# A list scheduler that bounds its stretches of small TensorE products by a time, and then keeps to full ones for a while

## The chip, the cores and the metric

The kernel runs on one core of one Trainium2 chip. The metric is the device time of one execution in microseconds; what stands for a kernel is the median of several runs. The five engines with a queue of their own are TensorE (PE in the profile, with the weight loads as PEld), VectorE (DVE), ScalarE (ACT), GpSimd (POOL) and SyncE (SP), which here only issues transfers.

## The reference

All data are float32, with one batch of 512 positions of width 1024. Two transformer layers follow each other:

```python
x = first_block(x, c, ...)        # adaLN; sparse attention + latent attention, gated; MLP, d_ff 4096
# second_block:
h = rmsnorm_2(x, norm_mix_g)
proj = h @ w_in                                          # 512 + 3*512 columns
y_ssm = s5_mixer(proj[..., :512], ...)                   # state-space scan, then a GLU
y_att = chunked_attention(q, k, v, rel_bias)             # 8 heads of 64
mixed = concat(rmsnorm_2(y_ssm, g1), rmsnorm_2(y_att, g2))
x = x + mixed @ w_out
h2 = rmsnorm_2(x, norm_ffn_g)
x = x + (silu(h2 @ w_gate) * (h2 @ w_up)) @ w_down       # d_ff 2816
return rmsnorm_2(x, norm_final_g)
```

The `s5_mixer` has 32 groups of 16 channels with 64 complex states each:

```python
bu = einsum('bsgh,gph->bsgp', uf, b_bar)
_, states = associative_scan(combine, (lam_bar, bu), axis=1)
y = einsum('bsgp,ghp->bsgh', states, c_mat).real + d_skip * uf
y = gelu(y); y = y * sigmoid(y @ w_glu + b_glu)
```

## The kernel before

**How products are made.** A large matrix product is kept at float32's precision by splitting both sides into a high and a low part (`hh`, `hl` for activations; `wh`, `wl` for weights) and adding three products: high by high, low by high, high by low. Weights stream through a ring of four buffers: a transfer on SP's queue brings a piece `wr` of 128x1024, ACT casts it to `wh`, and `Weights.low` (line 463) makes `wl = wr - wh`, on DVE, or on an engine that the scheduler chooses between DVE and POOL (`vg`). When `wl` is made, `Weights.freed` issues the transfer of the piece four further on, so that this transfer stands in SP's queue until that subtraction is done.

**The scan of the second block.** `ssm(hf)` (line 1990) is called for two halves of the channels. It loads 14 tables `rec` and the inputs `U`, makes for each of two sets `o` a bank T of 16 products with 64x64 tables (T<-U), which use a quarter of TensorE's array each, scans the result on DVE (`sr`, `st`, `ss`), and then makes two banks Y: 8 products T<-U of the full 128-row tables with 64 columns of output width and 16 products T<-ss, which contract over 64 rows only. These last and the 64x64 ones are called small here; PE's tiling then is (64, 64) or (64, 128) and not the full (128, 128). ACT copies the banks to `ye`; eight transfers on SP write it to `yd` in memory, two read it back transposed as `yt`, ACT copies each to `yy`, and a gelu follows on ACT and DVE (`yq`, `gl`). Its products with `w_glu` come after that, and then the output product with `in_w_out`, whose left side is `mxh`/`mxl` for the attention and `glh`/`gll` on the way of the scan.

**What runs beside it.** The projection `in_w_in` makes the columns of q, k, v (mm), and the eight attention heads run as chains: scores S, softmax `sb`, `st`, transposes T<-ident,sb, the pair `ph`/`pl`, the output O. POOL takes a chain of 16 steps on the residual `x` (scale and add) beside that. PSUM is divided into two banks for mm, three for S, two for T and one for O; the scan and the attention's transposes share the two T banks.

**What sets the order.** No order is written out. Every operation is recorded with a priority (`Plan`), `price` (line 130) gives it a cost and, for products, its tiling `mode`, and `Plan.schedule` (line 178) sorts the record: always the engine that is free first takes, of its ready operations, that with the best rank. At line 266 PE keeps its tiling: if the best operation has another tiling than the last, and one of the same tiling is ready within `STAY` = 120 ranks, that one is taken. A change of tiling is charged `SWITCH` = 0.2 us (line 306). So all small products that are ready within 120 ranks form one unbroken run. Operations recorded with an alternative (`alt`) go to whichever of two engines the simulated state favours, and a bank or buffer is given in the order of the simulated times: an edit of the rule on PE reorders other engines too. All operations are issued by one line of a helper, 377 before the change and 391 after it, so in the trace all rows have that line, and one goes by the names.

Of the kernel before, what the change touches and what calls it, by code (L numbers as in the profile page):

```python
# [29 lines left out]
for _name, _w in (("b_ada", 48), ("g_mix", 8), ("g_mlp", 8), ("g_final", 8), ("g_cq", 3), ("g_ckv", 2),  # L30
# [7 lines left out]
BGP = 300  # L38
SWITCH = 0.2
STAY = 120  # L40
ORDER = {"N": "Q3 Q2 V0 T0 Q1 V123 F T1 Q0 R S3 S2 S1 S0 T23",
         "M": "Q3 Q2 V0 T0 Q1 V123 F T1 Q0 T23",
         "2": "Q3 Q2 V0 T0 V123 F T1 Q1 Q0 T23"}
# [7 lines left out]
class Plan:  # L51
# [126 lines left out]
    def schedule(self, window):  # L178


        ops = self.ops
# [23 lines left out]
        order, done = [], [False] * n  # L205
# [5 lines left out]
        hw = dma = 0.0  # L211
        port = {"DVE": 0.0, "POOL": 0.0}
        other = {"DVE": "POOL", "POOL": "DVE"}
        mode = (128, 128)

        def offer(i):
            if rank[i] > front + window:
# [26 lines left out]
        while len(order) < n:  # L244
            best = None
            for e in self.eng:
                f, q = fut[e], rdy[e]
                while f and f[0][0] <= free[e]:
                    x = heapq.heappop(f)
                    heapq.heappush(q, (x[1], x[2]))  # L250
                s = free[e] if q else f[0][0] if f else None
# [4 lines left out]
            s, e = best  # L256
            f, q = fut[e], rdy[e]
            while f and f[0][0] <= s:
                x = heapq.heappop(f)
                heapq.heappush(q, (x[1], x[2]))  # L260
            r, i = heapq.heappop(q)
            o = ops[i]
            if done[i]:
                continue
            cost, fn = o.cost, o.fn
            if e == "PE" and o.mode != mode:

                near = min((x for x in q if x[0] < r + STAY and ops[x[1]].mode == mode and not done[x[1]]), default=None)
                if near is not None:
                    heapq.heappush(q, (r, i))  # L270
                    q.remove(near)
                    heapq.heapify(q)
                    r, i = near
                    o = ops[i]
                    cost, fn = o.cost, o.fn
# [27 lines left out]
                    slack[g][front:first[t]] -= 1  # L303
            end = s + cost
            if e == "PE":
                end += SWITCH * (o.mode != mode)
                mode = o.mode
            if o.port and e in port:
                port[e] = end
# [1 line left out]
            if o.nbytes:  # L311
# [7 lines left out]
                end = dma + 0.9  # L319
# [21 lines left out]
            for g in again:  # L341
                k = 0
                while wait[g]:
                    r, j = wait[g][0]
# [16 lines left out]
            while late and late[0][0] <= front + window:  # L361
                r, j = heapq.heappop(late)
# [161 lines left out]
def tile_kernel(ctx: ExitStack, tc: tile.TileContext, A, out):  # L524
# [845 lines left out]
    def pipeline(units, pre=None, ph=None):  # L1370
        n = len(units)
        at = lambda i: units[i] if 0 <= i < n else None
        for s in range(n + 2):
# [3 lines left out]
            later.flush()  # L1377
            for op in ORDER[ph].split():
                u = {"Q": a, "R": a, "S": a, "T": b, "V": c, "F": c}[op[0]]
# [900 lines left out]
```

## Time and profile before

| | |
|---|---|
| median of 3 runs | 1442.59 us (1439.56, 1442.59, 1442.77) |
| the profiled execution | 1439.8 us, with a span of 1437.7 us |
| mean granted TensorE clock | 0.991 of full speed |
| PE busy | 1402.6 us, 98% of the span |
| DVE, ACT, POOL busy | 937.2 us, 614.5 us, 137.3 us |
| the chain that ended last | PE 84% of the span, DVE 6%, ACT 3%, DMA 2%, issue 2%, POOL 2% |

The page gives busy time by engine and, in 40 slices, how it is spread. PE stands at 9 in all of them but one in the second half, where it is 8, and the last, where it is 6. The granted clock stands at 9 of 10 or more but in one slice of the second half. Slices are 36 us long, so that the views by window and the timelines of single engines tell more about that place; the rows read from them stand further below.

### The profile page before, as it was taken

What the parts mean: (1) busy time and instruction counts of PE and PEld (TensorE: products, weight loads), DVE (VectorE), ACT (ScalarE), POOL (GpSimd) and SP (SyncE); (2) the same over time, 40 slices, a digit from 0 to 9 for tenths busy, and PEclk for the clock granted to TensorE, in tenths of its full rate; (3) what the DMA queues carried; (4) which work ended last, traced back from release to release, by engine and by line L of the source; (5) the groups of instructions that cost most, each with busy time, mean ns of one, the idle gap of its engine ahead of it and who ended that gap; (6) DMA issues with size and microseconds to landing.
All of it is one profiled execution on the core that took longest, in us unless ns stands there. A gap on an engine that the chain in (4) does not pass through costs nothing.

```text
span 1437.7 us, 19122 instructions
## 1 busy us (share of the span) xinstructions
PE 1402.6 (98%) x7152; PEld 1173.3 (82%) x7152; DVE 937.2 (65%) x1830; ACT 614.5 (43%) x1065; POOL 137.3 (10%) x177
## 2 busy tenths in 40 slices
PE   9999999999999999999999999998999999999996
PEld 7889888877888888888888887886888888888885
DVE  6867777779887886946544656778776534553544
ACT  3435567667643442323324533767443312321322
POOL 1010001200000000000213121244300000000000
PEclk9999999999999999999999999998999999999999
DMA  9583453542264233244446666241233333333221
GB/s 365 183 304 102 141 156 138 161 140 59 82 200 145 59 110 97 88 126 131 142 149 189 216 231 133 70 133 48 75 93 97 92 105 98 88 103 117 88 59 59
DMA packets 73372, 185.81 MB, mean 129 GB/s; under 512 B 17048, under 2 KB 17896, under 8 KB 73280
## 3 DMA queue, kind: packets, MB, share of 16 engines
q1 hardware_dynamic: 64192, 159.67, 36.0%
q0 software_dynamic: 7552, 22.97, 5.0%
q10 hardware_dynamic: 1536, 1.95, 0.4%
q8 instruction: 56, 0.92, 0.3%
q14 instruction: 36, 0.29, 0.1%
HBM read 165.41 MB, written 19.67 MB: 129 GB/s over the span
## 4 chain that ended last, share of the span: by engine, by line
PE 84%; DVE 6%; ACT 3%; DMA 2%; issue 2%; POOL 2%; SPq 0%; DVEq 0%; POOLq 0%; ACTq 0%
PE mm L377 70%; PE T L377 5%; PE S L377 5%; PE O L377 3%; POOL x L377 1%; DMA adaw<-in_w_ada 1%; DVE sb L377 1%; DVE pl L377 1%; ACT sb L377 1%; DVE o L377 1%; ACT wh L377 1%; DVE xt L377 0%; DVE adacc L377 0%; DMA aw<-in_w_ada 0%; SPq L377 0%
## 5 line engine op out<-in xcount | busy, mean ns | idle before, releaser
L377 ACT CAST wh<-wr 128x1024 fp32r<-128x1024 f32 x209 | 219.8, 1051 | 380.5 <-PE mm L377 321.0
L377 PE MATMUL mm<-hh,wh 128*128 128x512 f32 x880 | 353.3, 402 | 3.7 <-ACT fm L377 1.9
L377 DVE TENSOR_TENSOR wl<-wr,wh 128x1024 fp32r<-128x1024 f32 x206 | 258.3, 1254 | 135.6 <-ACT wh L377 128.8
L377 PE MATMUL mm<-hl,wh 128*128 128x512 f32 x880 | 345.7, 393 | 0.0
L377 PE MATMUL mm<-hh,wl 128*128 128x512 f32 x880 | 345.4, 393 | 0.0
L377 PEld LDWEIGHTS mm<-hh,wl 128*128 128x128 f32 x880 | 165.3, 188 | 34.9 <-issue 0.2
L377 PEld LDWEIGHTS mm<-hh,wh 128*128 128x128 f32 x880 | 165.3, 188 | 34.4 <-issue 2.5
L377 PEld LDWEIGHTS mm<-hl,wh 128*128 128x128 f32 x880 | 165.7, 188 | 29.9
L377 PE MATMUL mm<-fh,wl 128*128 128x512 f32 x416 | 162.0, 390 | 0.0
L377 PE MATMUL mm<-fh,wh 128*128 128x512 f32 x416 | 162.0, 390 | 0.0
L377 PE MATMUL mm<-fl,wh 128*128 128x512 f32 x416 | 161.9, 390 | 0.0
L377 PEld LDWEIGHTS mm<-fh,wh 128*128 128x128 f32 x416 | 78.1, 188 | 16.5 <-issue 0.2
L377 PEld LDWEIGHTS mm<-fh,wl 128*128 128x128 f32 x416 | 78.1, 188 | 16.3
L377 PEld LDWEIGHTS mm<-fl,wh 128*128 128x128 f32 x416 | 78.1, 188 | 16.2
L377 ACT ACTIVATE sb<-sb,st 128x512 f32<-128x512 f32 (+3 forms) x128 | 71.5, 559 | 28.9 <-DVE st L377 26.7
L377 DVE TENSOR_TENSOR pl<-T,ph 128x384 fp32r<-128x384 f32 (+1 forms) x96 | 56.5, 595 | 21.5 <-ACT ph L377 16.0
L377 PE MATMUL T<-ident,sb 128*128 128x128 f32 x320 | 55.2, 280 | 5.9 <-DVE pl L377 2.8
L377 ACT CAST ph<-T 128x384 fp32r<-128x384 f32 (+1 forms) x96 | 48.1, 509 | 24.3 <-PE T L377 23.4
L377 DVE CUSTOM_DVE_ANT_0 sb<-S,nb 128x256 f32<-128x256 f32 (+2 forms) x96 | 44.9, 484 | 15.6 <-PE S L377 15.3
L377 PEld LDWEIGHTS T<-ident,sb 128*128 128x128 f32 x320 | 39.5, 143 | 18.1 <-issue 4.0
L377 DVE TENSOR_TENSOR swg<-mm,R 128x512 f32<-128x512 f32 x21 | 14.5, 691 | 60.9 <-PE mm L377 60.9
L377 ACT ACTIVATE sw<-swg 128x512 f32<-128x512 f32 x22 | 13.9, 631 | 83.4 <-DVE swg L377 83.4
(376 smaller groups left out, 2357.0 us busy)
## 6 DMA issues: line engine op xcount, KB each, us to landing
wr<-in_w_fc SPq DMA_DIRECT2D x64, 512.0 KB, 3.6
wr<-in_w_in SPq DMA_DIRECT2D x48, 512.0 KB, 4.0
wr<-in_w_gu SPq DMA_DIRECT2D x44, 512.0 KB, 3.6
adaw<-in_w_ada POOLq DMA_DIRECT2D x32, 512.0 KB, 5.0
wr<-in_w_down SPq DMA_DIRECT2D x22, 512.0 KB, 3.5
aw<-in_w_ada SPq DMA_DIRECT2D x32, 256.0 KB, 6.6
wr<-in_w_out SPq DMA_DIRECT2D x16, 512.0 KB, 3.9
rec<-srec SPq DMA_DIRECT2D x28, 256.0 KB, 6.5
```

The lines of the kernel that those rows point to most:

```text
L377: fn(*o.a, **o.kw)
```

## The change

Two constants come in, `SMALL` = 1.3 and `DENSE` = 2.0, in the scheduler's own microseconds. While PE is in a small tiling and has been for more than `SMALL`, the scheduler wants a full product: if one is ready within `STAY` ranks, it is taken although a small one has a better rank. If that change was made so (`broke`: a full product came after more than `SMALL` of a small tiling), PE keeps to full products for as long as `DENSE`, as before whenever one is ready, and after that takes the operation with the best rank, whatever its tiling. In all other cases the rule is the one of before.

```diff
+SMALL, DENSE = 1.3, 2.0
@@ Plan.schedule
-        mode = (128, 128)
+        mode = full = (128, 128)
+        since, broke = 0.0, False
@@
-            if e == "PE" and o.mode != mode:
-                near = min((x for x in q if x[0] < r + STAY and ops[x[1]].mode == mode and not done[x[1]]), default=None)
+            if e == "PE":
+                small, other_ = mode != full, o.mode != mode
+                if small and s - since > SMALL and not other_:
+                    want = full
+                elif other_ and not (broke and s - since > DENSE):
+                    want = mode if not (small and s - since > SMALL) else None
+                else:
+                    want = None
+                near = None if want is None else min((x for x in q if x[0] < r + STAY and ops[x[1]].mode == want
+                                                      and not done[x[1]]), default=None)
                 if near is not None:
@@
             if e == "PE":
-                end += SWITCH * (o.mode != mode)
+                if o.mode != mode:
+                    end += SWITCH
+                    broke = o.mode == full and s - since > SMALL
+                    since = s
                 mode = o.mode
```

No operation is added, taken away or changed in size; only their order, and for some the engine, differs.

The first place is PE at the first 32 small products of the scan, the two T banks of the first half (T_1896 and T_1905). `mm_1907` is the projection in progress. Before:

```order
L377 MATMUL mm_1907<-wl_1866,hh_1812 128x256
L377 MATMUL T_1896<-U_1889,rec_1879 64x64 x8
L377 MATMUL T_1896<-U_1889,rec_1881 64x64 x8
L377 MATMUL T_1905<-U_1889,rec_1880 64x64 x8
L377 MATMUL T_1905<-U_1889,rec_1882 64x64 x8
L377 MATMUL mm_1907<-wh_1868,hh_1820 128x256
```

And in the same place of the changed kernel:

```order
L391 MATMUL T_1896<-U_1889,rec_1879 64x64 x8
L391 MATMUL T_1896<-U_1889,rec_1881 64x64 x2
L391 MATMUL mm_1907<-wh_1868,hh_1820 128x256
L391 MATMUL mm_1907<-wh_1868,hl_1821 128x256
L391 MATMUL mm_1907<-wl_1869,hh_1820 128x256
L391 MATMUL mm_1907<-wh_1868,hh_1828 128x256
L391 MATMUL mm_1907<-wh_1868,hl_1829 128x256
L391 MATMUL mm_1907<-wl_1869,hh_1828 128x256
L391 MATMUL mm_1907<-wh_1868,hh_1839 128x256
L391 MATMUL mm_1907<-wh_1868,hl_1840 128x256
L391 MATMUL mm_1907<-wl_1869,hh_1839 128x256
L391 MATMUL T_1896<-U_1889,rec_1881 64x64 x6
```

The run of 32 is cut after ten products; nine products of the projection stand between it and the next, which is of ten too (four of T_1905 follow in it), and the rest of T_1905 comes later still, in two more pieces.

The second place is DVE at the end of the stretch, where q and k of the last pair of heads are made (`qk`, `qA`, `k2l`), and the two weight splits `wl_2261` and `wl_2274` stand between them. Before:

```order
L377 TENSOR_TENSOR qA_2171<-qk_1633_2169,qA_2171 64x512
L377 TENSOR_TENSOR wl_2261<-wr_2094,wh_2260 128x1024
L377 TENSOR_TENSOR qk_1637_2176<-mm_2172,R_1360_1851 128x512
L377 TENSOR_TENSOR wl_2274<-wr_2101,wh_2273 128x1024
L377 TENSOR_TENSOR k2l_2178<-qk_1637_2176,k2A_2177 64x512
L377 TENSOR_TENSOR pl_2191<-T_2189,ph_2190 128x512
```

And after:

```order
L391 TENSOR_TENSOR qA_2171<-qk_1633_2169,qA_2171 64x512
L391 TENSOR_TENSOR qk_1637_2176<-mm_2172,R_1360_1851 128x512
L391 TENSOR_TENSOR pl_2191<-T_2189,ph_2190 128x512
L391 TENSOR_TENSOR k2l_2178<-qk_1637_2176,k2A_2177 64x512
L391 TENSOR_TENSOR k2l_2180<-qk_1637_2176,k2A_2179 64x512
```

The two splits are gone from DVE. They stand on POOL instead, the third place, at the end of its chain on the residual, where nothing stood between that chain and `rs_2287` before:

```order
L391 TENSOR_SCALAR x_1757_2302<-x_1757_2302,vec 128x512
L391 TENSOR_TENSOR x_1756_2301<-x_1756_2301,R_1849 128x512
L391 TENSOR_TENSOR x_1757_2302<-x_1757_2302,R_1849 128x512
L391 TENSOR_TENSOR wl_2274<-wr_2101,wh_2273 128x1024
L391 TENSOR_TENSOR wl_2261<-wr_2094,wh_2260 128x1024
L391 TENSOR_TENSOR rs_2287<-ms_2286,mhalf 128x4
```

The two have changed places with each other too. The transfers that need their buffers, `wr_2262` and `wr_2275`, stand in SP's queue where they stood, among the eight writes of the scan's output (`ye_2089` is the second half's) and ahead of the two reads:

```order
L377 DMA yd<-ye_2089 16x16x64 x6
L377 DMA wr_2262<-in_w_out 128x1024
L377 DMA yd<-ye_2089 16x16x64
L377 DMA wr_2275<-in_w_out 128x1024
L377 DMA yd<-ye_2089 16x16x64
L377 DMA yt_2167<-yd 128x512
L377 DMA yt_2168<-yd 128x512
```

These rows on SP read the same in both kernels but for the line number; the engine that releases the two loads is now POOL.

## Rows read from the trace of the kernel before

**Rows 1.** Page, part 1: busy us, share of the span, instructions.

```profile
PE 1402.6 (98%) x7152; PEld 1173.3 (82%) x7152; DVE 937.2 (65%) x1830; ACT 614.5 (43%) x1065; POOL 137.3 (10%) x177
```

**Rows 2.** Busy time of each engine in three windows; the first line names the columns.

```profile
core 0: us, PE busy (x) PEld busy (x) DVE busy (x) ACT busy (x) POOL busy (x), PEclk, DMA share, GB/s
870.60:873.70 3.10, 0.26 (x3) 0.06 (x2) 1.23 (x1) 1.04 (x1) 0.00 (x0) 1.00 1.08 208
892.00:936.00 44.00, 40.67 (x342) 35.46 (x341) 32.19 (x82) 31.57 (x70) 10.36 (x17) 1.00 0.30 81
977.30:1008.00 30.70, 24.35 (x113) 18.20 (x111) 23.83 (x48) 23.75 (x49) 9.15 (x5) 0.83 0.20 56
```

**Rows 3.** Timeline of PE around 875; the first line names the columns.

```profile
start us, us, engine line op out<-in xcount [idle before <-releaser]
873.73 3.00 PE L377 MATMUL T<-U,rec 128*64 128x64 f32 x64 [2.87 <-DMA wr<-in_w_in]
...
877.04 0.41 PE L377 MATMUL mm<-wh,hl 128*128 128x256 f32 x1
877.25 0.41 PE L377 MATMUL mm<-wl,hh 128*128 128x256 f32 x1
...
878.19 0.28 PE L377 MATMUL mm<-wh,hl 128*128 128x256 f32 x1
878.31 0.28 PE L377 MATMUL mm<-wl,hh 128*128 128x256 f32 x1
```

**Rows 4.** One more window, the same columns as in the first windows.

```profile
874.50:878.00 3.50, 3.50 (x51) 3.38 (x48) 2.94 (x12) 0.00 (x0) 0.00 (x0) 0.51 1.46 124
```

**Rows 5.** Timeline of PE around a run of 16 small products.

```profile
897.94 0.34 PE L377 MATMUL S<-k2A,qA 128*128 128x384 f32 x1
898.12 0.34 PE L377 MATMUL S<-k2l,qA 128*128 128x384 f32 x1
898.39 2.00 PE L377 MATMUL T<-ss,rec 64*128 64x64 f32 x32
900.32 0.50 PE L377 MATMUL mm<-hh,wh 128*128 128x512 f32 x1
900.66 0.40 PE L377 MATMUL mm<-hl,wh 128*128 128x512 f32 x1
```

**Rows 6.** Timeline of PE, two waits for DVE in the second half.

```profile
919.60 0.69 PE L377 MATMUL T<-U,rec 128*64 128x64 f32 x16 [0.59 <-DVE pl L377]
...
921.85 0.52 PE L377 MATMUL T<-ident,sb 128*128 128x128 f32 x3 [0.68 <-DVE st L377]
```

**Rows 7.** Timeline of DVE, the two weight splits and a later wait.

```profile
975.49 2.21 DVE L377 TENSOR_TENSOR wl<-wr,wh 128x1024 fp32r<-128x1024 f32 x1
...
978.22 1.71 DVE L377 TENSOR_TENSOR wl<-wr,wh 128x1024 fp32r<-128x1024 f32 x1
...
986.65 0.56 DVE L377 TENSOR_TENSOR pl<-T,ph 128x384 fp32r<-128x384 f32 x1 [1.05 <-POOL x L377]
```

**Rows 8.** Timeline of POOL: one weight split, and steps on the residual.

```profile
939.67 2.40 POOL L377 TENSOR_TENSOR wl<-wr,wh 128x1024 fp32r<-128x1024 f32 x1
959.83 3.11 POOL L377 TENSOR_SCALAR x<-x,vec 128x512 f32<-128x512 f32 x2 [17.76 <-DMA x<-x1d]
...
978.83 3.06 POOL L377 TENSOR_SCALAR x<-x,vec 128x512 f32<-128x512 f32 x1
...
985.32 1.30 POOL L377 TENSOR_TENSOR x<-x,R 128x512 f32<-128x512 f32 x1
```

**Rows 9.** Timeline of SP's queue, and from the issues: KB, us to landing.

```profile
977.73 0.35 SPq L377 DMA_DIRECT2D wr<-in_w_out  x1
...
980.35 0.43 SPq L377 DMA_DIRECT2D yd<-ye  x1
984.77 0.81 SPq L377 DMA_DIRECT2D yt<-yd  x2
...
yt<-yd SPq DMA_DIRECT2D x4, 256.0 KB, 2.8
```

**Rows 10.** Timeline of ACT, the second copy of what was read back.

```profile
996.89 1.15 ACT L377 COPY yy<-yt 128x512 f32<-128x512 f32 x1
```

**Rows 11.** Timeline of PE where its full stream begins again.

```profile
1008.00 0.50 PE L377 MATMUL mm<-glh,wh 128*128 128x512 f32 x1 [0.15 <-ACT gt L377]
```

## The prediction

> **What bounds the kernel now.** I read the page first: PE is busy 98% of a span of 1437.7 us [rows 1]. So a microsecond put on PE is a microsecond of time, except where PE waits, and only there can an order gain. I built the changed kernel and compared the orders: all engines stand as before up to the state-space stage of the second block and again after its output product, so the question lies in one stretch, 870 to 1010 us, under a tenth of the span. I took the busy time of each engine in pieces of it [rows 2]. PE idles 2.8 us in 870.6 to 873.7 (the input of the scan is loaded), 3.3 us in 892 to 936, and 6.4 us in 977.3 to 1008, where the last two attention heads and the second half of the scan's output come to their end together. Between these pieces it is full. That is the most the change can win by filling: some 9 us, since the load at 870.6 is untouched. Within the stretch the clock stands at 2.4 GHz but for 1.2 GHz from 874.5 to 878 [rows 4], and for a part of the last 30 us (mean 0.83) [rows 2].
>
> **What the change does to the order.** Products on a part of the array (the scan's 64x64 and 64x128 ones) stood in 7 unbroken runs, of 32, 24 and 8 products and four of 16. They now stand in 21 runs of 10 or fewer, with a few full products between. The scheduler's bound is 1.3 us of its own reckoning, but in the trace 32 products of the 64x64 kind, two instructions each, take 3.00 us, part of it at the low clock [rows 3], and 16 of the other kind, 32 instructions, take 2.00 [rows 5], so that a run of ten or five is really near 0.6 us.
>
> **Cost of more runs.** I take the run at 898.39 [rows 5]. The product of 384 columns ahead of it starts at 898.12 and such a one takes 0.18 (897.94 to 898.12), so the run could have begun at 898.30: 0.09 lost. Its last instruction begins at 898.39 + 2.00 - 0.27 = 900.12, one every 0.056, and the next full product begins at 900.32: 0.14 lost. That one and its successor are 0.34 apart where 0.23 is usual: 0.11. Together 0.34 a run, and 14 runs more: 14 x 0.34 = +4.8 us, on PE where it is full. Where the neighbour is another f32 product the 0.11 falls away: 14 x 0.23 = 3.2 is the lower bound. For the upper one I let each end of a run wait for the 0.27 us that one product takes less its 0.056: 14 x (0.43 + 0.11) = 7.6. The Trainium skill says in "TensorEngine Tiling (Array Packing)", Key Properties, that changing the tiling mode, not just the tile, drains the engine. By the page each end would cost such a drain and the sum would be the 7.6; the row, with 0.09 and 0.14, says less, and I go by the row.
>
> **The low clock at 874.5.** The wait of 2.8 us ahead of it stays, the clock stood at 2.4 GHz in the first of the small products, and it fell within a microsecond of their start [rows 2 to 4]. Elsewhere runs of 2.00 us leave it alone: it is 1.00 in 892 to 936 [rows 2, 5]. So I read the idle time as the cause and leave the fall in. What runs under it changes: before mostly small products, now twelve full ones of 256 columns in place of six. Such a one takes 0.21 at 1.2 GHz and 0.12 at 2.4 [rows 3]: 6 x 0.09 = 0.5, less 0.1 for small products moved out: +0.4 us. Bounds: -0.9 (no fall) and +1.
>
> **Waits inside the stretch.** Two banks of PSUM serve the scan, its transposes and the attention's. In 919 to 922 PE waits 0.59 and 0.68 for DVE to read a bank [rows 6]; there the new order puts transposes between the pieces, and of the idle 3.3 us I take 1.4 as gone, about these two. New is that a bank stays open longer: the first half's second product group is completed three runs later, its readers on DVE stand behind a weight split and the first group's whole scan, and the group that wants the bank next follows five small and two full products later. No row of before shows that wait; I give it 0.7, the size of the larger one of rows 6. Sum -0.7; bounds -3.3 (every idle microsecond of 892 to 936 filled) and +2 (none gone, three such waits new).
>
> Up to the last projection that feeds the last two heads (977.3 us) this makes 4.8 + 0.4 - 0.7 = **+4.5 us**.
>
> **The last 30 us.** Here the diff says nothing and the order says much: the low parts of two weight pieces (wl_2261, wl_2274) leave DVE, and stand on POOL behind its sixteen steps on the residual (x). Two sides follow.
>
> The attention's side gains. On DVE the two took 2.21 and 1.71 us between the projection's end and the heads' scores, and the next bank read waited another 1.05 for POOL, whose scaling row it shared a buffer with; that wait is gone too [rows 7]. Against casts on ACT that cover part of it I take -2.8, and -1.1 for one copy (yy) that now stands behind the transposes. 1008.0 + 4.5 - 3.9 = 1008.6 for the time at which PE resumes full work (before, 1008.00 [rows 11]).
>
> The scan's side loses. SP's queue is the same row by row: six writes of the scan's output, a weight load, the seventh, a weight load, the eighth, then the two reads back (yt). Each of those two loads needs the buffer that a wl frees. Before, DVE freed them: the first load went at 977.73, the eighth write, behind the second, at 980.35, and the read at 984.77, 4.4 us on [rows 9]. Now POOL frees them. Its chain on x ended at 985.32 + 1.30 = 986.6 [rows 8]; its loads move with PE by half of the 4.5 (+2.2), and it runs beside a DVE without the two wl: -1.5 from the step at 978.83, which took 3.06 beside them where a pair took 3.11 before [rows 8], and -1.0, an estimate, for the step ahead of it. 986.3, then 2 x 2.40 [rows 8] = 991.1, the queue's 0.4 and 4.4, the landing's 2.8 (yt's median [rows 9]): the output is back at 998.7 instead of 987.6. ACT takes it in order. In the trace the second copy began at 996.89 and PE resumed at 1008.00: 11.1 us with the same thirteen steps behind it that stand there now [rows 10, 11]. With the first copy's 1.1: 998.7 + 12.2 = 1010.9. The later side decides: 1010.9 - 1008.0 = **+2.9 us**. Behind 1008 PE is full again and nothing gives it back.
>
> **Against what.** The profiled execution took 1439.8 (span 1437.7 and 2.1 around it), so the sum gives 1442.7. The three runs of before lie at 1439.56 to 1442.77, median 1442.59, 2.8 above it; why they differ no trace shows, and I put the difference on the median: 1442.59 + 2.9 = 1445.5.
>
> **Rivals.** *Slower by more: the late read-back decides alone.* POOL slows when DVE works beside it (the step at 978.83 took twice the usual [rows 8]), the wl there would take, at a quarter more, 3 us each and x start with all of the 4.5 late. The output then lands at 998.7 + 1.2 + 2.3 = 1002.2, PE resumes at 1014.4, +6.4: 1449. It decides as soon as the output lands later than 996.4, where both sides meet, and each microsecond beyond is one of time. For it speaks that POOL is busy 9 us beyond 977.3 already [rows 2]; against it, that ACT has less else to do by then and may need fewer than 12 us.
>
> *Faster: dense work between the runs pays.* Runs cost the lower bound (3.2), the idle time of 892 to 936 is filled (-3.3), the clock does not fall at 874.5 (-0.9), the heads' side gains its 3.9 and POOL comes early enough: -4.9, or 1437.7. The skill's "TensorE: Matmul & The Clock Gate", Part 1, says that the throttled state is the default and activity releases it; by that rule small products could count for little and the change would be right in its aim. The page's result would be this rival's. What speaks against it in rows are runs of 2.00 us at an unmoved clock.
>
> *Nothing: what is lost on PE is taken from waits.* Extra runs fill the idle 3.3 us and the heads' 3.9, and both sides still meet at 1008 to 1009: 0 to +1, 1443.
>
> **How the numbers follow.** About 0.3%, 4.3 us, can be told from no change here: faster is under 1438.3, slower over 1446.9. The forecast (1441.5 to 1448) has 0.50, of it 0.04 over 1446.9; the late read-back 0.26; dense work 0.15, of it 0.01 within; nothing 0.09. So faster 0.14, same 0.46 + 0.09 + 0.01 = 0.56, slower 0.30. The range reaches to 1437.5, the faster rival's own time, and to 1450, a microsecond past the slower one's; beyond it I leave some 0.1 on either side.
>
> **What would show it.** In the changed kernel's profile: runs of ten products of 0.5 to 0.6 us with 0.2 to 0.35 lost around each; the clock still at 1.2 GHz from about 874.5; a wait of PE for DVE in the first half's third or fourth run; the two wl on POOL behind x, SP's weight load with them, and yt landing near 999; ACT waiting for it, and PE resuming its full stream near 1011. I am wrong if the read-back lands before 996 and the heads still end late (then the runs cost more than 0.34), if the clock stays at 2.4 GHz through 874 to 878, or if PE's idle time in 892 to 936 goes to nothing.

## The result and the profile after

The changed kernel takes 1452.16 us, the median of 19 runs (1447.43 to 1461.68), against 1442.77 of the kernel before in 19 runs beside it (1437.51 to 1450.48). The ratio is 1.0063, with a 95% interval of 1.0048 to 1.0078: 9.4 us slower, where +2.9 was forecast; the time lies above the stated range, which ended at 1450.

The profiled execution has a span of 1445.6 us, against 1437.7, at the same mean clock (0.991). Its busy times, page part 1, answer to [rows 1]:

```profile
PE 1408.3 (97%) x7152; PEld 1175.7 (81%) x7152; DVE 937.2 (65%) x1828; ACT 613.9 (42%) x1065; POOL 139.8 (10%) x179
```

The work is the same and PE is busy 5.7 us longer. Both kernels run the same 900 instructions of PE from the scan's first product to the first output product (mm<-mxh); I call this the stretch. It took 140.42 us before and takes 149.03; behind it PE needs 412.6 us to the end of its last product in both. It falls into four stages at points that both orders share: up to the second half's first 64x64 product (T<-U), up to the end of the scan's last product, up to the heads' last part, and that last part. Windows of the kernel before, with the columns of [rows 2]:

```profile
873.73:917.86 44.13, 43.40 (x325) 37.38 (x325) 30.68 (x75) 21.20 (x43) 6.91 (x11) 0.96 0.43 88
917.86:961.26 43.40, 40.63 (x350) 36.24 (x349) 35.41 (x92) 28.35 (x60) 12.50 (x15) 1.00 0.35 107
961.26:977.90 16.64, 16.64 (x94) 13.79 (x92) 12.75 (x24) 11.09 (x24) 16.64 (x12) 1.00 0.27 80
977.90:1014.15 36.25, 29.90 (x139) 22.89 (x138) 28.46 (x54) 28.32 (x57) 8.55 (x5) 0.86 0.22 62
```

The same stages of the changed kernel:

```profile
872.98:922.05 49.07, 48.26 (x324) 39.24 (x324) 30.75 (x78) 20.69 (x43) 4.47 (x8) 0.97 0.35 79
922.05:974.88 52.83, 49.09 (x378) 42.06 (x378) 36.66 (x90) 29.50 (x62) 25.12 (x26) 1.00 0.33 106
974.88:985.75 10.87, 10.87 (x65) 9.23 (x64) 9.60 (x22) 10.16 (x22) 10.70 (x8) 1.00 0.20 38
985.75:1022.01 36.26, 28.28 (x139) 22.15 (x138) 30.36 (x53) 27.84 (x56) 6.53 (x3) 0.91 0.22 62
```

The first stage loses 4.9 us with the same products in it and hardly more idle time. The second and third have to be taken together, since the scan's end comes later among the others: 60.04 before, 63.70 now, +3.7. The last stage, on which the prediction spent most of its words, takes the same 36.26 us. That it is the same is in part luck: PE idled more (8.0 us against 6.4), and the clock stood better (0.91 against 0.86).

To see what the loss is made of, I took for each step from one product to the next its excess over what the same form usually takes at 2.4 GHz in the kernel before, and added these up by what the step is. The last line is what is left, so that the five add up to the stretch:

| excess in the stretch, us | before | after | difference |
|---|---|---|---|
| ends of small runs (entry, leaving, the full product behind) | 2.33 | 6.63 | +4.30 |
| between T<-ss products inside a run | -0.02 | 2.58 | +2.60 |
| PE idle | 9.85 | 12.53 | +2.68 |
| all steps under the 1.2 GHz clock | 7.02 | 5.17 | -1.85 |
| everything else | 121.24 | 122.12 | +0.88 |

The second line was in no term of the prediction. It is plain in PE's timeline of the changed kernel; the run at 886.62 answers to the one in [rows 5]:

```profile
882.29 1.32 PE L391 MATMUL T<-ss,rec 64*128 64x64 f32 x10
...
886.29 0.40 PE L391 MATMUL mm<-hh,wh 128*128 128x512 f32 x1
886.62 1.33 PE L391 MATMUL T<-ss,rec 64*128 64x64 f32 x10
887.87 0.50 PE L391 MATMUL mm<-hl,wh 128*128 128x512 f32 x1
888.21 0.39 PE L391 MATMUL mm<-hh,wl 128*128 128x512 f32 x1
```

Its ends cost what was read before: 0.10 on entry, and 0.34 from the full product behind to its successor. But ten instructions take 1.33 us, where [rows 5] has 32 in 2.00. Those ran in twos: a product of the first bank on the lower 64 rows of the array and one of the second bank on the upper, whose instructions start 0.007 apart, with 0.105 to the next two. The changed order takes five products of the first bank (T_1914) at 882.29, because the second's (T_1915) full products have not been made yet, and at 886.62 five of the second, whose partners are gone by then. In both runs the instructions start 0.112 apart: one without a partner takes as long as two. Counted in the order, 24 products T<-ss stand without a partner now, and none did before. The 64x64 products T<-U, which the section on the kernel says use a quarter of the array, contract over all 128 rows (128*64 in the views), so they use a half of it, and their tiling is (128, 64); they stand in pairs of left and right halves in both orders, and none is alone.

The Trainium skill says in "TensorEngine Tiling (Array Packing)", Key Properties, that different tiles can work in parallel. The trace agrees, with 0.112 us for one instruction or two. It follows that a tiling into halves is worth nothing where neighbours use the same half.

### The profile page after: what moved, and what is told of

It is laid out like the page before. It is cut to its first block, busy times and chain, and to the rows that moved or that the text cites. A ratio compares the mean times of both kernels' runs of the same rounds, so it can differ in the third digit from the quotient of the medians.

```text
span 1445.6 us, 19115 instructions
## 1 busy us (share of the span) xinstructions
PE 1408.3 (97%) x7152; PEld 1175.7 (81%) x7152; DVE 937.2 (65%) x1828; ACT 613.9 (42%) x1065; POOL 139.8 (10%) x179
## 4 chain that ended last, share of the span: by engine, by line
PE 86%; DVE 6%; ACT 3%; DMA 2%; issue 1%; SPq 0%; DVEq 0%; POOLq 0%; POOL 0%; ACTq 0%
PE mm L391 71%; PE T L391 6%; PE S L391 5%; PE O L391 4%; DVE sb L391 1%; DMA wr<-in_w_in 1%; DVE pl L391 1%; DVE wl L391 1%; ACT sb L391 1%; DMA adaw<-in_w_ada 1%; ACT wh L391 1%; DVE o L391 1%; DVE xt L391 0%; DVE adacc L391 0%; DMA aw<-in_w_ada 0%
## 5 line engine op out<-in xcount | busy, mean ns | idle before, releaser
L391 DVE TENSOR_TENSOR wl<-wr,wh 128x1024 fp32r<-128x1024 f32 x204 | 253.1, 1241 | 140.2 <-ACT wh L391 138.1
L391 DVE TENSOR_TENSOR pl<-T,ph 128x384 fp32r<-128x384 f32 (+1 forms) x96 | 56.5, 596 | 25.0 <-ACT ph L391 23.3
```

The lines of the kernel that those rows point to most:

```text
L391: fn(*o.a, **o.kw)
```

## Experiments

The measure, beside the ratio, is the stretch of each profile. A ratio here is uncertain by some 3 us, and the stretch by what the clock does in that one execution, so each is read with the excess by kind of step.

**Lone products, 56.** In the kernel before, each run of T<-ss is sorted by bank:

```diff
+                new = sorted((order[at[j]] for j in range(k, m)),
+                             key=lambda x: self.box(self.ops[x[1]].a[1])[0])
```

> The kernel before, with one edit: in each of its four runs of 16 products T<-ss, all eight of the first bank come first and then all eight of the second, where they alternate otherwise. Runs, engines and all other rows stay. The measure is the stretch on PE from the scan's first product to the first output product (mm<-mxh): 140.4 us before, 149.0 in the changed kernel. Theory A: two of these products, on the two halves of the array's rows, run side by side, and one without a partner takes as long as a pair (0.112 us more in the trace of the changed kernel); 14 of 16 in each run now have none, 56 in all: +6.3 us, a stretch of 146.7. Theory B: only the changes between small and full products cost time; there are as many as before: 140.4.

The ratio is 1.0065 (1.0028 to 1.0101). Here is its first run, in PE's timeline:

```profile
896.20 3.39 PE L378 MATMUL T<-ss,rec 64*128 64x64 f32 x32
```

And the 17 us before and behind a point just after it, as windows:

```profile
882.70:899.80 17.10, 17.10 (x104) 14.82 (x104) 15.11 (x35) 7.31 (x12) 3.70 (x5) 1.00 0.30 89
899.80:916.90 17.10, 17.10 (x69) 15.18 (x69) 2.20 (x9) 3.71 (x12) 0.57 (x1) 0.50 0.18 47
```

3.39 in place of 2.00 with the clock at 2.4 GHz, +1.4 for 14 lone products: theory A, at 0.10 each. But the stretch is 157.66, 11 more than that gives, since right behind this run the clock fell to 1.2 GHz for 17 us, and again for 17 us at 971.5. Neither theory had that.

The ratio doesn't price the lone products either. The mean granted clock of each run tells why: it is 0.981 on average over these six, and 0.9877 over the 93 runs of the kernel before that stand beside the experiments. That is 20 us more at 1.2 GHz, where work takes up to twice as long (0.21 us against 0.12 for a product of 256 columns, [rows 3]): an estimate of up to 10 us, and the six are 10.8 us slower on average.

**Shorter runs, all pairs kept.** In the kernel before, the T<-ss runs are cut:

```diff
+                runs = [seq[j:min(j + piece, m)] for j in range(k, m, piece)]     # piece = 4
+                for p, r in enumerate(runs):
+                    out += r
+                    if p < parts:
+                        out += take[p * n // parts:(p + 1) * n // parts]          # full ones that follow
```

> The kernel before, with its four runs of 16 products T<-ss cut into pieces of four (twice) or of four and eight, and one or two of the full products that follow put between the pieces: 16 runs in place of 7, every pair kept, all other rows as they were. Theory A and theory B (a change costs 0.34 us, of 0.09 on entry, 0.14 on leaving and 0.11 in the full pair behind): 9 x 0.34 = +3.1 us, a stretch of 143.5. Rival C: the changes cost nothing, only lone products and waits do: 140.4.

The ratio is 1.0081 (1.0054 to 1.0107), the stretch 153.28: far over both. The test was not clean. The scores S, taken forward, waited 1.3 us for ACT's k2A, and the clock stood at 1.2 GHz for 17 us amid the first half's runs and for 10 in the second half. It was no chance of this profile: all six runs have a mean clock of 0.978 to 0.983, below every one of the 93 of the kernel before (0.984 to 0.992). At 2.4 GHz its entries cost 0.15 each and its exits 0.17, a little over the price. The same cut for the 64x64 runs alone:

```diff
-PIECE, FULL, CUTMODES = 4, 2, ((64, 128),)
+PIECE, FULL, CUTMODES = 4, 2, ((128, 64),)
```

> The kernel before, with the runs of 64x64 products T<-U cut into pieces of four (the 32 into eight, the 24 into five, the 8 into two) and one or two of the full products that follow put between: 19 runs in place of 7, every pair kept, the 64-row products and all other engines as they were. By the price of a change read from rows (0.09 on entry, 0.12 on leaving a 64x64 run, 0.10 in the full pair behind): 12 x 0.31 = +3.7 us, a stretch of 144.1, or 143.6 where a single full product stands between two pieces and the last part falls away. Rival: the changes of tiling cost nothing by themselves: 140.4. Rival of the clock: with a full product every few small ones the granted clock stays at 2.4 GHz behind the scan's first products, and 1 us comes back.

The ratio is 1.0041 (1.0019 to 1.0063), the stretch 150.18, and again it is the clock: 1.2 GHz from 878.3 for 17 us, where the unbroken run of the kernel before had 3.4. The rival of the clock is refuted, by its opposite: full products put between small ones did not keep the clock up here. The ten runs say so too, with 0.984 on average, 11 us more at 1.2 GHz than the kernel before. Why pieces of four pull the clock down is open.

**24 lone products in unbroken runs.** As the first experiment, but only for the first eight products of each run:

```diff
+                new[:8] = sorted(new[:8], key=lambda x: self.box(self.ops[x[1]].a[1])[0])
```

> The kernel before, with only the first eight products of each run of 64-row ones reordered (four of the first bank, then four of the second): 24 lone products, as many as in the changed kernel, in the 7 runs of before. By the price of a lone product (0.112 us): +2.7, a stretch of 143.1 if the granted clock stays, and no loss of the clock behind the runs. Rival of the clock: as in the run with 56 lone products, the clock falls to 1.2 GHz behind one or two of the runs for some 17 us, and the stretch is 148 or more.

Each run takes 2.50 us in place of 2.00, four times, and the excess inside them is +1.97 (2.7 expected). The clock did not fall behind the runs, nor at the scan's start, and the stretch is 140.42, just that of before: the missing fall at the scan's start gives back 1.7 us and less idle time 0.4. The ratio, 0.9991 (0.9974 to 1.0008), does not show the 2 us; its interval ends at +1.2. So the price of a lone product is shown by rows, in three kernels, and by no time.

**The changed kernel with pairs kept.**

```diff
-                if small and s - since > SMALL and not other_:
+                if small and s - since > SMALL and not other_ and odd % 2 == 0:
@@ ssm: the first T<-ss product of a bank waits for the last T<-U product of both banks
+                        if k + w + e == 0:
+                            both.succ.append(plan.ops[-1])
+                            plan.ops[-1].npred += 1
```

> The changed kernel with pairs kept: a run of small products ends only after an even number of them, and the 64-row products of a bank wait until those of its partner can be taken too. 19 runs in place of 21, no lone product in place of 24. Theory A: 24 x 0.112 = 2.7 us for the pairs and 2 x 0.34 = 0.7 for the runs come back: a stretch of 149.0 - 3.4 = 145.6, within 1 us for waits that move. Theory B: 148.3.

The ratio is 1.0008 (0.9988 to 1.0028): nearly all of the loss is gone, with 19 runs. The stretch is 143.94, less than expected. Inside the T<-ss runs no excess is left (-0.03), and the ends of runs cost 6.58 where the kernel before has 2.33: 4.25 for 12 more, 0.35 each. In this order, though, the two weight splits came back to DVE by themselves, which the expectation had not allowed for. So the next two part the one from the other.

**The splits back on DVE, the pairs lost.** In `Weights.low` of the changed kernel:

```diff
+        if l.tensor.name.endswith(('_2261', '_2274')):
+            self.plan.ops[-1].alt = None
```

> The changed kernel with the two weight splits wl_2261 and wl_2274 made on DVE, as before the change; PE's 21 runs and 24 lone products stay. The prediction's theory (POOL's late splits hold SP's loads, the read-back yt comes late and sets the end): the read-back lands some 10 us earlier, only the heads' side is left, and the stretch falls by 2 us or more, to 147 or less. Theory now (ACT reached the read-back's copies late for the heads' sake, and DVE lost as much time beside POOL as the splits would have taken it): 149.0, within 1 us.

The stretch is 145.74, the number of the prediction's theory: the splits' place is worth 3.3 us in this profile. What makes it so is not the read-back, though: it does not land 10 us earlier but is issued 2.6 us later than in the changed kernel's 996.53, in SP's timeline:

```profile
999.16 0.81 SPq L391 DMA_DIRECT2D yt<-yd  x2
```

The ratio, 1.0048 (1.0020 to 1.0077), does not part it from the changed kernel's 1.0063.

**The splits on POOL, the pairs kept.** The kernel with pairs kept, and the two splits put on POOL:

```diff
+            o = self.plan.ops[-1]
+            o.eng, o.fn, o.cost = o.alt
+            o.alt = None
```

> The changed kernel with pairs kept (19 runs, none lone), but with the two weight splits on POOL, where the run with pairs kept has them on DVE; else as that run. It parts the two things that the run with pairs kept did at once. If the splits' place is what it won (2 us of waits in the tail): a ratio of 1.005 to the kernel before, level with the changed kernel. If the pairs are (24 lone products, 2.6 us, and 2 runs, 0.6): 1.001 to 1.003, as with pairs kept.

The ratio is 1.0052 (1.0028 to 1.0077). The first three stages repeat those with the splits on DVE to within 0.03 us; the last one differs. Here are the last stages with pairs kept and the splits on DVE, with pairs kept and the splits on POOL, and of the changed kernel with the splits on DVE, one line from each kernel:

```profile
986.50:1020.24 33.74, 27.86 (x139) 21.78 (x138) 28.53 (x55) 27.60 (x56) 2.85 (x2) 0.90 0.24 68
```

```profile
987.53:1024.14 36.61, 29.85 (x139) 22.99 (x138) 29.65 (x53) 27.78 (x56) 7.77 (x4) 0.86 0.21 62
```

```profile
988.61:1021.14 32.53, 26.72 (x140) 20.94 (x137) 28.41 (x55) 27.69 (x56) 1.39 (x1) 0.95 0.24 71
```

With the splits on DVE the last stage takes 33.7 or 32.5 us, with them on POOL 36.6 or 36.3. Between the two with pairs kept, some 0.9 of it is idle time and 2 are products under the lower clock, which stood there for longer. By ratios (1.0008 and 1.0052, from two comparisons) the place is worth 0.4%, which by the expectation's rule speaks for the place and against the pairs. But of these 4 us most is again the clock: it is 0.9885 on average over the runs with the splits on DVE and 0.9863 with them on POOL, 6.6 us less at 1.2 GHz, or some 3 us of time. The ratio with the splits on POOL is not told from the changed kernel's 1.0063, so no time shows what keeping the pairs is worth. The stretch does: it is 146.78, with 3.4 us more at 1.2 GHz than in the changed kernel's first profile. At the same clock that makes about 145.1, near the 145.6 that the 24 pairs and 2 runs were priced at.

What the place costs is in the timelines of POOL, DVE and PE of the changed kernel:

```profile
987.12 5.16 POOL L391 TENSOR_TENSOR wl<-wr,wh 128x1024 fp32r<-128x1024 f32 x2
...
987.41 5.42 DVE L391 TENSOR_TENSOR k2l<-qk,k2A 64x512 fp32r<-64x512 f32 x2
...
993.60 0.67 PE L391 MATMUL O<-ph,V 128*128 128x512 f32 x1 [2.23 <-DVE o L391]
```

DVE's two k2l steps, which the last heads' scores need, take 5.42 us beside the two splits. With the splits on DVE (pairs kept) the same two are these, in DVE's timeline:

```profile
990.55 0.68 DVE L391 TENSOR_TENSOR k2l<-qk,k2A 64x512 fp32r<-64x512 f32 x1
...
991.86 0.69 DVE L391 TENSOR_TENSOR k2l<-qk,k2A 64x512 fp32r<-64x512 f32 x1
```

The splits went away from DVE, 2 x 1.22 us there, and took 5.42 - 1.37 = 4.05 of its time nevertheless. In five profiles a k2l meets a split on POOL, eight times in all, and each time it ends 0.55 us behind the end of the split. The Trainium skill says in "SBUF — State Buffer", Who interferes with whom, that a DVE instruction with two SBUF inputs contends with a GpSimd instruction that reads SBUF, and that the pair of ports the two share is an exclusive lock. The trace agrees, with the 4.05 us and the eight ends.

**The splits on POOL in the kernel before.** The same edit there:

> The kernel before, with the two weight splits wl_2261 and wl_2274 made on POOL in place of DVE; the 7 runs stay, and behind the second half's scan the order of some heads' products follows. If the splits' place is worth in the tail what the changed kernel gained by having them back on DVE (3.3 us of its stretch): 143.7, with a DVE instruction of two SBUF operands that lasts 2 us or more beside a split on POOL. Rival: that gain belonged to the clock and to the late scan, and the place alone costs nothing: 140.4, within 1 us.

The rival holds: the stretch is 141.35, with 10 us at 1.2 GHz in its first stage that the first profile of before lacks, and the ratio 0.9977 (0.9957 to 0.9997), a gain if anything. Its last stage takes 33.31 us against 36.25. Here one k2l came just before the splits and the other 6 us later, and they took 0.68 and 1.02 us, the second because it began 0.47 us ahead of a split's end. So it is not POOL that costs, but what DVE has to do beside it.

**Runs bounded at 2.6, pairs kept.**

```diff
-SMALL, DENSE = 1.3, 2.0
+SMALL, DENSE = 2.6, 2.0
```

> The changed kernel with pairs kept and the bound SMALL at 2.6 in place of 1.3: 12 runs, none lone, where 1.3 with pairs gave 19. By the price of a run (0.31 us): 5 runs more than before the change cost +1.6 us of the stretch, 7 fewer than at 1.3 give back 2.2; 142.0 where the clock and the waits are as before, and a time within 0.3% of before. Rival of the clock: longer runs lose the clock more often than at 1.3, and the time is above that with 19 runs.

The ratio is 1.0033 (1.0012 to 1.0053), the stretch 145.94. With 12 runs the ends cost 4.25, 2.3 less than with 19, as priced. But PE idles 15.1 us in place of 11.3, 4.1 of them in the first half of the scan where the other has 1.9. Behind the scan's products it idles 8.3 in place of 5.9; there this order has one of the two splits on POOL, where the other has both on DVE, and a k2l of 2.75 us beside it. Which waits an order makes is not told by its count of runs.

**A version against both.** The wait at the scan's start is there in both kernels (2.87 us in [rows 3], and 2.50). In the kernel before, the scheduler reckons 3 us more for the loads of U:

```diff
-                end = dma + 0.9
+                end = dma + 0.9 + o.lag          # 3.0 for the loads of U, else 0
```

> The kernel before, whose scheduler reckons 3 us more for the loads of the scan's input U: 14 full products of 256 columns stand ahead of the scan's first products and no longer behind them; runs and all other engines but for seven rows of DVE stay. If PE's wait of 2.9 us at the scan's start is one for U: 14 x 0.12 = 1.7 us of it are filled, and the whole time falls by 1 to 2 us. Rival: the wait is one for the weights of those 14 products, which land no earlier: no gain.

The ratio is 0.9943 (0.9920 to 0.9965), from four runs, and in its profile PE doesn't wait ahead of the scan (1.2 us, for DVE, come 4 us later). That was more than the wait is worth, so it was run again:

> The kernel before with 3 us more reckoned for the loads of U, once more and in more runs, since the first time had four and its profile lost 14 us of the stretch to the 1.2 GHz clock: 14 products of 256 columns fill the wait ahead of the scan, 1.7 us, and a ratio of 0.9985 if that is all. The first time's ratio of 0.994 holds only if fuller work ahead of the scan also keeps the clock up in most executions.

With 12 runs it is 0.9982 (0.9963 to 1.0002): the 0.9985 of the wait alone. Their mean clock is 0.9877, that of the kernel before; the first four had 0.9898. It is clearly faster than the changed kernel, and not clearly faster than the one before. With the bounded runs and their pairs it did not add up:

> The changed kernel with pairs kept (as in the run with pairs kept) and 3 us more reckoned for the loads of U (as in the run with a late U): 18 runs, none lone, no wait at the scan's start. If the two edits add up: level with the kernel before (1.001) for the first, 0.6% for the second, so a ratio of 0.995 to the kernel before. If bounding the runs keeps the clock at 2.4 GHz where the unbroken runs lose it (some 10 us at 1.2 GHz behind the second run in two profiles): lower than the late U alone, 0.992 or less. Rival: the late U's gain was chance, or its cover is used by the bounded runs: 1.001.

The ratio is 1.0033 (1.0006 to 1.0059), with 14 us at 1.2 GHz from 894.5 in its profile: neither 0.995 nor less, and the rival's 1.001 is nearest.

**The clock by itself.** Both kernels were profiled once more, unedited:

> The kernel before once more, unedited, for a second profile of it: where the granted clock falls in the stretch. If the fall behind its unbroken runs of 64-row products is a matter of chance, as rows of four kernels with that same order suggest (none, 3, 10 and 10 us at 1.2 GHz), it may be there in this one and was not in the first; the runs themselves, 1.73 us from their first to their last instruction at 2.4 GHz, are the same.

> The changed kernel once more, unedited, for a second profile: 20 changes more cost the same (entry 0.09, exit 0.14, the pair behind 0.11 at 2.4 GHz), 24 lone products 2.6 us, POOL's splits hold k2l on DVE for 4 us or more, and the stretch is 149.0 but for what the clock does. If the gap between the medians (9.4 us) is more than that between the profiles (7.6) because the clock falls more often in the changed kernel, this profile shows more than the 10 us at 1.2 GHz of the first in its stretch; if it is chance, the same or less.

Their stretches are 145.10 and 157.04, 4.7 and 8.0 us longer than in the first profiles, in the same order of instructions. In the second profile of the changed kernel the two k2l beside POOL's splits take 4.51 us, 3.1 more than alone. Windows of the kernel before behind its first run of T<-ss, the second profile and then the same place in the first:

```profile
899.40:909.60 10.20, 10.20 (x52) 8.68 (x52) 1.30 (x6) 2.05 (x7) 0.00 (x0) 0.50 0.18 38
```

```profile
897.03:907.23 10.20, 10.20 (x78) 8.79 (x78) 3.86 (x13) 4.93 (x14) 1.61 (x3) 1.00 0.25 47
```

And of the changed kernel in its second half, the second profile and then the same place in the first:

```profile
967.30:984.40 17.10, 17.10 (x71) 14.07 (x70) 0.26 (x1) 1.61 (x4) 16.93 (x13) 0.50 0.19 66
```

```profile
964.70:981.80 17.10, 17.10 (x117) 14.08 (x116) 6.47 (x17) 7.91 (x21) 16.93 (x13) 1.00 0.32 91
```

The clock falls or doesn't behind the same instructions. In the stretch it stood at 1.2 GHz for 13.6 and 23.3 us in the two profiles of before, and for 10.2 and 30.7 in those of after. Whether it does so more often in the changed kernel, two profiles each can't tell, but the mean clocks of all runs bound it: 0.9870 over the 19 of the changed kernel against 0.9877. That is 2 us more at 1.2 GHz, uncertain by some 5: about 1 us of the 9.4. The gap between the medians is in the main not the clock's.

## Why the prediction was wrong, step by step

- **The bound.** Right: the whole difference lies in the stretch, and PE's 412.6 us behind it are the same.
- **Cost of more runs.** The size of what was priced held: +4.3 us of ends in the profile, where +4.8 stood (0.31 to 0.35 a run in place of 0.34). Beside the scan's own full products 0.05 of the 0.11 stays, where the lower bound had it fall away. The step failed by what it left out: it took the inside of a run as unchanged. The row it used (32 instructions in 2.00 us) hid that they run in twos, and the order of the changed kernel, which it had at hand, has five products of one bank in a row. The term it lacks is 24 x 0.11 = 2.6 us.
- **The low clock at 874.5.** It fell there in the changed kernel's first profile (from 874.3, 3.4 us) and not in its second (885.4), nor in six of the experiments, whose PE waited 1.6 to 2.8 us at the same place. So the reading that the idle time makes the clock fall was too strong as a certainty. It isn't refuted: over the 13 profiles with these loads of U, PE waited 2.4 to 3.6 us there in the six where the clock fell, and 1.6 to 2.8 in the seven where it didn't, and in the second profile of before it fell 0.6 us ahead of the first small product.
- **Waits inside the stretch.** -0.7 was forecast up to the projection's end. The two waits of [rows 6] did go, and others came:

```profile
923.82 0.52 PE L391 MATMUL T<-ident,sb 128*128 128x128 f32 x3 [0.71 <-DVE pl L391]
...
936.11 0.63 PE L391 MATMUL T<-ident,rw 128*128 128x128 f32 x4 [1.57 <-DVE pl L391]
```

  PE idles 1.0 us more there, not 0.7 less: the new wait is of the kind that was expected (a T bank held longer), at twice its size and in the second half. With the scan's start 0.75 earlier, 4.3 + 2.6 + 1.0 - 0.75 gives 7.2 of the 7.85 us by which the last stage began late, where +4.5 was forecast; the rest is spread over the other products.
- **The last 30 us.** Forecast -1.6, came 0, in part by luck: the clock stood at 1.2 GHz for 6.8 us there in place of 10.2, worth some 1.7 us. The scan's side was right in its times and wrong in its weight. The read-back was issued at 996.53, and with 2.8 us to landing it is there at 999.3 (forecast 998.7); but ACT, held by the heads' steps ahead of it, took it at 1004.25, in SP's and ACT's timelines:

```profile
996.53 0.82 SPq L391 DMA_DIRECT2D yt<-yd  x2
...
1004.25 2.12 ACT L391 COPY yy<-yt 128x512 f32<-128x512 f32 x2
```

  The heads' side was wrong: the splits were to leave DVE 2.8 us to the good, and DVE stood still beside them for 4.05, as much as the 2.21 and 1.71 that they took on DVE before. The prediction had a sign of this in its own rows: the two are the same subtraction, which takes 1.22 us in the kernel with pairs kept; in [rows 7] both take longer, beside POOL's steps on x. It named POOL as slowed by DVE, but not DVE by POOL.
- **Against the median.** 2.8 was put between the profile and the median for both. Over 19 runs it is 3.0 before (1442.77 - 1439.8) and 4.7 after (1452.16 against 1447.43, the run whose span is the profile's). The clock moves single executions by that much. Both profiles fell in executions with a better clock (0.991) than the average of their kernel's runs (0.9877 and 0.9870); why the difference is 1.9 us larger after the change is not shown.
- **Rivals.** The slower one, with its 1449, had the sign and the wrong mechanism. Dense work between the runs did not pay.

So the 6.7 us by which the forecast was too low are 2.6 for lone products, 1.6 for the last stage, 1.7 for waits, 1.9 for the median, less 0.5 at the ends of runs and 0.6 of the rest, the scan's earlier start above all. The first three are read from the rows and stages of one profile; the ratios alone do not part them.

## What to carry to other kernels

Before pricing a reordering by the ends of runs, look at what neighbours inside a run do for each other: products on the two halves of TensorE's array go in pairs, and a scheduler that cuts a run by time must cut it after a whole pair and only with both banks open. When a step of two SBUF operands moves from DVE to POOL, see what DVE does at that moment; if it also reads two SBUF operands, the step takes its time from DVE all the same. Where the clock falls in some executions and not in others, one profile gives a difference of some us no sign: compare the excess of single kinds of steps at one clock, and the mean clock of all runs to see whether an order loses the clock more often.

## What was not expected of the hardware

A 64-row f32 product of 64 columns takes 0.112 us for each of its two instructions whether the other half of the array works or not. DVE's k2l took 5.42 us for two beside POOL's splits, and 0.68 each alone. And the granted clock fell to 1.2 GHz for 3.4 to 17 us behind stretches of small products in some executions and stayed at 2.4 in others of the same kernel. Cutting the runs finer, into pieces of four products, made it worse: 0.980 and 0.984 on average over the runs of the two kernels, where the kernel before has 0.9877.
